# A two-layer decoder on one core: the FFN's 256-column chunk with gate and up in one matmul, two new banks for the last columns, and another order of the attention steps

## The chip, the cores and the metric

The kernel runs on one core of one Trainium2 chip. The metric is the device time of one execution in microseconds (us); lower is better. Engines are named as in the profile: PE (TensorE matmuls), PEld (its weight loads), DVE (VectorE), ACT (ScalarE), POOL (GpSimd), SP (SyncE, which issues most DMAs).

## What is computed

```python
for i in range(2):                      # x: 256 tokens x 1024
    h = rmsnorm(x, norm_mix[i]); mem_n = rmsnorm(mem, norm_mem[i])
    mix, mem_q = gmlp_mixer(h, ...) if i == 0 else nsa_mixer(h, ...)
    mem_o = mem_cross_attention(mem_q, mem_n, w_mem_kv[i])   # 4 heads, 256 memory tokens
    x = x + concatenate([mix, mem_o]) @ w_out
    h = rmsnorm(x, norm_ffn[i])
    x = x + (silu(h @ wg[i]) * (h @ wu[i])) @ wd[i]          # d_ff 2816
return rmsnorm(x, norm_final)
```

All data are float32. Layer 0 mixes tokens with a gated MLP (gMLP), whose spatial weights are 12 causal 128x128 matrices; layer 1 has attention (NSA) with 12 heads in 4 groups and three gated branches: compressed blocks, selected blocks and a window.

## The kernel before

A float32 matmul is made of three passes of a faster type. Every operand is split into a high part H and the rest L, and `mm3` (L228 to L230) adds aH·bH, aL·bH and aH·bL in one PSUM bank. `split` makes the high part on ACT (L122) and the rest on DVE (L123). So each piece of a weight (1024 columns) costs ACT one `wH` and DVE one `wL`, and each activation an `aH` and an `aL`. In the trace, H and L of an attention or FFN result are written `aH`, `aL` or `mid`.

Weights come as tiles of 1 MB (`Raw`, three buffers) from DMAs that SP issues. There are seven buffers each for `wH` and `wL`: a piece can be split when the piece seven before it has had its last use, which is in token block 1 (`tb`, 128 tokens each; there are two).

PE runs its program in the order in which the code issues it. This order is written by hand: `flow` advances a clock by an estimate for each matmul, and a spawned chain that says `yield 2.4` goes on when that clock is 2.4 us later. ACT, DVE and POOL run what a tile scheduler ordered by priority; `tc.high_priority(offset=...)` moves what is issued in it ahead.

The parts that the change touches:

- **FFN.** 2816 hidden columns in six chunks: first the 256 columns from 2560, then five of 512. For each chunk and token block `gate` multiplies into one bank and takes SiLU from it (L447, ACT); `up` multiplies into another and spawns `turn`, which takes the product (L451, DVE), transposes it after `yield 1.6` (L244, x2 or x4) and splits it. `down` then adds the chunk to four accumulators (2 token blocks x 2 halves of 512 columns) that stay open over all chunks. In the first chunk the order is gate, up for block 0, then gate, up for block 1.
- **Attention.** For each of six head pairs m there are three steps: `scores` (L925 to L929, then maxima on DVE, exponentials on ACT at L949, scaling on POOL at L954 and DVE), `turn` (12 transposes of probabilities and one of the compressed ones, `pcx`, L244; then copies L974, L980, L983 on ACT), and `attend` (L1001, with the split `aH`, `aL` of its result). `mixed(m, tb)` multiplies a finished result with its part of the output weights (two halves, 3 passes each; the `mm` tiles in lines L228 to L230 of the profile) and adds to accumulators of the next residual.
- **Compression** (layer 1): two hidden layers; SiLU of the first (L808, ACT), `yield 3.0`, two transposes, the second layer.
- **gMLP**: `v_chain` transposes the spatial weights (L660 and L661, three sets of four groups), then mixes set by set (`spatial`, L639); `yield 0.8` stands behind each set of transposes.
- **Memory attention**: copies of transposed probabilities on ACT (L412).
- **The end**: `final` adds the residual (L306, DVE), takes the sum of squares (L249, ACT), multiplies with the norm's weights (L1085, DVE), and when both halves are there takes the reciprocal root (L257, L258, POOL), scales (L1092 DVE, L1094 ACT) and stores with two DMAs of SP (L1095).

Of the kernel before, what the change touches and what calls it, by code (L numbers as in the profile page):

```python
# [11 lines left out]
AF = mybir.ActivationFunctionType  # L12
ALU = mybir.AluOpType
# [4 lines left out]
D = 1024  # L18
# [39 lines left out]


HI = 150  # L60
MEMLAT = 9.0
MEMCH = 0.0
VCH = 2.0
# [4 lines left out]
def body(tc, t, out):  # L68
    nc = tc.nc
    PE, ACT, DVE, POOL, SP = nc.tensor, nc.scalar, nc.vector, nc.gpsimd, nc.sync  # L70
    with ExitStack() as ctx:
# [233 lines left out]
            xs = x[:, tb, half * 512 : (half + 1) * 512]  # L305
            DVE.tensor_tensor(xs, acc, xs, op=ALU.add)  # L306

        def down(accs, act, ks, ws, first, last, after=None, tbs=(0, 1)):

            for tb in tbs:  # L310
                for half in range(2):
                    acc = accs[tb][half]
                    for i, k in enumerate(ks):
                        mm3(acc, st(act, k, tb), ws[i](slice(half * 512, (half + 1) * 512)),
                            first and i == 0, last and i == len(ks) - 1)
                        if tb == 1 and half == 1:
                            ws[i].done()
                    if after:
                        after(acc, tb, half)
# [61 lines left out]
        def mem_attention(qTs, tb, kv, dst, done):  # L381
# [26 lines left out]
            for i in range(2):  # L408
                pt = tr()
                transposes(pt, parts[i].rearrange("p j n -> p (j n)"), 4)  # L410
                pT = small([128, 4, 128])
                ACT.copy(pT, kview(pt, 4))  # L412
                pTs.append(pT)
            yield 3.2
            o = tr()
# [11 lines left out]
        def ffn_weights(layer):  # L427
            wg, wu, wd = t["ffn_w_gate"][layer], t["ffn_w_up"][layer], t["ffn_w_down"][layer]
            out = []
            for c0, n in [(2560, 256)] + [(i * 512, 512) for i in range(5)]:  # L430
                out.append((n // 128, w_in(wg, c0, n), w_in(wu, c0, n),
                            sum([cols(wd, c0 // 128 + k, 2, 0, D) for k in range(0, n // 128, 2)], [])))
            return out

        def ffn(weights, nrm, after):
            accs = [[mm(), mm()], [mm(), mm()]]
            for ci, (nk, wg, wu, wd) in enumerate(weights):
                n = nk * 128
                sil = [None, None]
                act = mid([128, 4, SEQ], F32R), mid([128, 4, SEQ], F32R)  # L440

                def gate(tb):
                    ps = tr()
                    gemm(ps, nrm.act, tb, wg, n)
                    sil[tb] = small([128, n])
                    with tc.high_priority(offset=HI):
                        ACT.activation(sil[tb], ps[:, :n], AF.Silu, scale=nrm.rstd[tb])  # L447

                def turn(ps, tb, act=act, sil=sil, n=n, nk=nk):
                    h = small([128, n])  # L450
                    DVE.scalar_tensor_tensor(h, ps[:, :n], nrm.rstd[tb], sil[tb], op0=ALU.mult, op1=ALU.mult)  # L451
                    yield 1.6
                    pt = tr()
                    transposes(pt, h, nk)
                    split(act[0][:, :nk, blk(tb)], act[1][:, :nk, blk(tb)], kview(pt, nk))

                def up(tb):
                    ps = tr()
                    gemm(ps, nrm.act, tb, wu, n)
                    flow.spawn(turn(ps, tb))  # L460
                    flow.tick(0)

                for f, tb in ((gate, 0), (up, 0), (gate, 1), (up, 1)) if nk == 2 else ((gate, 0), (gate, 1), (up, 0), (up, 1)):
                    f(tb)
                last = ci == len(weights) - 1
                end = lambda *a: flow.spawn(after(*a))
                down(accs, act, range(nk), wd, ci == 0, last, end if last else None)
            return accs


# [177 lines left out]
        def v_chain():  # L648
# [9 lines left out]
            for q in range(3):  # L658
                ps = tr()
                transposes(ps, wsr[:, q * 4 : q * 4 + 4, :].rearrange("p g s -> p (g s)"), 4)  # L660
                ACT.copy(wsT[:, q * 4 : q * 4 + 4, :], kview(ps, 4))  # L661
                yield 0.8
            for q in range(3):
                spatial(q)
                yield 1.0
# [98 lines left out]
        def compress():  # L764
# [41 lines left out]
            POOL.memset(hS, 0.0)  # L806
            for s in range(2):
                ACT.activation(hS[s * 64 : s * 64 + 60, :], ph[s * 64 : s * 64 + 60, 0:256], AF.Silu)  # L808
            yield 3.0
            pt = tr()  # L810
            transposes(pt, hS, 2)
            hTk = small([128, 2, 60])
# [173 lines left out]
        def attend(m):  # L986
            pT0, pT1 = turned[m]
            o = tr()
            for tb in range(2):
                n = 3 if tb == 0 else 5  # L990
                for i in range(n):
                    for hh in range(2):
# [6 lines left out]
                        else:  # L999
                            w, z = V[:, i // 2, i % 2, c], pT1[hh][:, i, :]  # L1000
                        PE.matmul(o[hh * 64 : hh * 64 + 64, blk(tb)], w, z, start=i == 0, stop=i == n - 1)  # L1001
            split(mix1[0][:, m, :], mix1[1][:, m, :], o[:, 0:256])

        soft, turned = {}, {}

# [7 lines left out]


        def step(f, *a):
            with tc.high_priority(offset=HI):
                f(*a)

        ps = mm()
# [35 lines left out]
        step(turn, 2)  # L1055
        mixed((1, 0))
        step(scores, 4)
        mixed((0, 1))
        step(attend, 2)
        step(turn, 3)  # L1060
        mixed((2, 0))
        step(scores, 5)
        mixed((1, 1))
        step(attend, 3)
        step(turn, 4)
        mixed((3, 0))
        step(attend, 4)
        step(turn, 5)
        mixed((4, 0), (2, 1))
        step(attend, 5)  # L1070
        mixed((3, 1), (5, 0), (4, 1), (5, 1))
        flow.until(lambda: f1.rstd[0] is not None)
# [2 lines left out]
        SP.dma_start(nf, t["norm_final"].partition_broadcast(128))  # L1075
        oview = out[0].rearrange("(b p) d -> p b d", p=128)
        sse = [tiny([128, 2], "ss") for _ in range(2)]

        def final(acc, tb, half):

# [15 lines left out]
            return  # L1096
            yield

        xgs = []
        ffn(WF1, f1, final)  # L1100
        flow.until(lambda: len(xgs) == 4)


_INS = [
# [33 lines left out]
```

## Time and profile before

| | |
|---|---|
| median of 3 runs | 637.43 us (636.39 to 638.38) |
| the profiled execution | 638.98 us, of which its span is 637.3 us |
| mean granted TensorE clock in it | 0.994 |
| PE busy | 97% of the span |

The span is the time from the first to the last record of the profile; the rest of the execution's time lies around it. [...] A matmul's duration in a row is longer than its pitch, the time from its start to the next one's start, since matmuls overlap in the engine.

### The profile page before, as it was taken

The numbers are of one execution on the slowest core, as the hardware profiler recorded it, in microseconds if no ns is written. First come the engines' busy times: TensorE is split into PE (matmuls) and PEld (weight loads), VectorE is DVE, ScalarE is ACT, GpSimd is POOL, SyncE is SP. The second block draws the span as 40 slices with busy tenths as digits, with TensorE's granted clock in tenths as the row PEclk, the third lists the DMA queues.
The fourth block names the chain that finished last, engine by engine and source line by source line (L and its number), as shares of the span: only waits on it lengthen the run. The fifth ranks groups of instructions, "written<-read, shape, count | busy, mean of one in ns | idle before, by whom it ended". The sixth has DMA issues, their size and how long they took to land.

```text
span 637.3 us, 8843 instructions
## 1 busy us (share of the span) xinstructions
PE 618.8 (97%) x3382; PEld 512.1 (80%) x3382; DVE 377.1 (59%) x616; ACT 327.0 (51%) x553; POOL 58.1 (9%) x90
## 2 busy tenths in 40 slices
PE   8999999999999999999999999889999999999995
PEld 6879879888888888889876786668988888888884
DVE  4898457463645545476597489746644545546344
ACT  5785567443535344365544479746543535344333
POOL 0330111000000000002003106420000000000001
PEclk9999999999999999999999999989999999999998
DMA  7966254565555564744948552042554554636401
GB/s 239 374 225 230 74 190 141 198 202 192 162 188 182 172 224 136 260 132 121 354 140 273 123 134 61 8 145 87 198 181 150 205 191 162 234 134 231 163 0 66
DMA packets 57330, 109.69 MB, mean 172 GB/s; under 512 B 3428, under 2 KB 19400, under 8 KB 57288
## 3 DMA queue, kind: packets, MB, share of 16 engines
q1 hardware_dynamic: 57272, 109.12, 51.4%
q8 instruction: 26, 0.43, 0.3%
q14 instruction: 16, 0.13, 0.1%
q10 hardware_dynamic: 16, 0.00, 0.0%
HBM read 108.07 MB, written 1.05 MB: 171 GB/s over the span
## 4 chain that ended last, share of the span: by engine, by line
PE 84%; ACT 5%; DMA 4%; DVE 4%; issue 1%; POOL 1%; SPq 0%; POOLq 0%; ACTq 0%; DVEq 0%
PE tr L229 13%; PE mm L228 13%; PE mm L229 13%; PE tr L230 13%; PE tr L228 13%; PE mm L230 12%; PE tr L244 4%; ACT mid L949 3%; DMA wsr<-in_gmlp_w_s_dram 2%; DMA x<-in_x_dram 1%; PE tr L798 1%; DVE wL L123 1%; DMA raw<-in_w_mem_kv_dram 1%; DVE wL L128 1%; PE tr L388 1%
## 5 line engine op out<-in xcount | busy, mean ns | idle before, releaser
L123 DVE TENSOR_TENSOR wL<-raw,wH 128x1024 fp32r<-128x1024 f32 (+1 forms) x170 | 207.0, 1236 | 148.8 <-ACT wH L122 142.9
L122 ACT CAST wH<-raw 128x1024 fp32r<-128x1024 f32 (+1 forms) x170 | 173.8, 1043 | 150.3 <-PE tr L229 75.5
L228 PE MATMUL tr<-wH,aH 128*128 128x512 f32 (+1 forms) x384 | 143.8, 375 | 0.0
L229 PE MATMUL tr<-wH,aL 128*128 128x512 f32 (+1 forms) x384 | 142.8, 372 | 0.6 <-DVE aL L123 0.6
L230 PE MATMUL tr<-wL,aH 128*128 128x512 f32 (+1 forms) x384 | 142.7, 372 | 0.0
L228 PE MATMUL mm<-wH,aH 128*128 128x512 f32 (+2 forms) x224 | 87.4, 390 | 0.0
L229 PE MATMUL mm<-wH,aL 128*128 128x512 f32 (+2 forms) x224 | 83.4, 372 | 3.3 <-DVE aL L123 3.3
L230 PE MATMUL mm<-wL,aH 128*128 128x512 f32 (+2 forms) x224 | 83.3, 372 | 0.1
L229 PEld LDWEIGHTS tr<-wH,aL 128*128 128x128 f32 x384 | 72.4, 188 | 13.1 <-DVE aL L123 0.9
L230 PEld LDWEIGHTS tr<-wL,aH 128*128 128x128 f32 x384 | 72.3, 188 | 12.6
L228 PEld LDWEIGHTS tr<-wH,aH 128*128 128x128 f32 x384 | 72.3, 188 | 12.3
L228 PE MATMUL mm<-wH,mid 128*128 128x512 f32 (+1 forms) x208 | 79.2, 381 | 0.0
L229 PE MATMUL mm<-wH,mid 128*128 128x512 f32 (+1 forms) x208 | 77.9, 374 | 0.0
L230 PE MATMUL mm<-wL,mid 128*128 128x512 f32 (+1 forms) x208 | 77.8, 374 | 0.0
L228 PEld LDWEIGHTS mm<-wH,aH 128*128 128x128 f32 x224 | 42.6, 190 | 10.2 <-issue 4.5
L229 PEld LDWEIGHTS mm<-wH,aL 128*128 128x128 f32 x224 | 42.5, 190 | 9.8 <-DVE aL L123 4.2
L230 PEld LDWEIGHTS mm<-wL,aH 128*128 128x128 f32 x224 | 42.4, 189 | 7.8 <-DVE wL L128 0.5
L257 POOL TENSOR_SCALAR rstd<-ss 128x1 f32<-128x1 f32 x14 | 7.4, 526 | 435.4 <-ACT junk L249 431.2
L230 PEld LDWEIGHTS mm<-wL,mid 128*128 128x128 f32 x208 | 39.2, 188 | 7.1
L229 PEld LDWEIGHTS mm<-wH,mid 128*128 128x128 f32 x208 | 39.2, 189 | 6.9 <-DVE mid L123 0.5
L228 PEld LDWEIGHTS mm<-wH,mid 128*128 128x128 f32 x208 | 39.2, 188 | 6.7 <-ACT mid L122 0.4
L451 DVE SCALAR_TENSOR_TENSOR small<-tr,rstd,small 128x512 f32<-128x512 f32 (+1 forms) x24 | 16.9, 703 | 36.5 <-PE tr L230 36.5
(158 smaller groups left out, 649.9 us busy)
## 6 DMA issues: line engine op xcount, KB each, us to landing
raw<-in_ffn_w_down_dram SPq DMA_DIRECT2D x22, 1024.0 KB, 5.0
raw<-in_ffn_w_gate_dram SPq DMA_DIRECT2D x20, 1024.0 KB, 5.1
raw<-in_ffn_w_up_dram SPq DMA_DIRECT2D x20, 1024.0 KB, 5.1
raw<-in_nsa_w_in_dram SPq DMA_DIRECT2D x6, 1024.0 KB, 6.9
raw<-in_gmlp_w_in_dram SPq DMA_DIRECT2D x4, 1024.0 KB, 8.7
raw<-in_w_mem_kv_dram SPq DMA_DIRECT2D x4, 1024.0 KB, 5.8
raw<-in_gmlp_w_out_dram SPq DMA_DIRECT2D x4, 1024.0 KB, 6.7
raw<-in_nsa_w_out_dram SPq DMA_DIRECT2D x12, 256.0 KB, 5.0
```

What stands on the lines that cost most here:

```text
L122: ACT.copy(H, src)
L123: DVE.tensor_tensor(L, src, H.bitcast(F32), op=ALU.subtract)
L128: DVE.scalar_tensor_tensor(L, src, g, H.bitcast(F32), op0=ALU.mult, op1=ALU.subtract)
L228: PE.matmul(ps, aH, bH, start=first, stop=False)
L229: PE.matmul(ps, aL, bH, start=False, stop=False)
L230: PE.matmul(ps, aH, bL, start=False, stop=last)
L244: PE.transpose(ps[:, (at + j) * 128 : (at + j + 1) * 128], src[:, j * 128 : (j + 1) * 128], ident)
L257: POOL.tensor_scalar(r, ss[:, 0:1], ss[:, 1:2], EPS, op0=ALU.add, op1=ALU.add)
L388: PE.matmul(scs[i][:, j * 256 : (j + 1) * 256], qT[r, j, :], kv[r, j, :], start=True, stop=True)
L451: DVE.scalar_tensor_tensor(h, ps[:, :n], nrm.rstd[tb], sil[tb], op0=ALU.mult, op1=ALU.mult)
L798: PE.matmul(ph[s * 64 : s * 64 + 60, 0:256], X[s][:, k // 8, k % 8, :], w1[q, s][:, j, :], start=k == 0, stop=k == 15)
L949: ACT.activation(o, o, AF.Exp, bias=nb[:, i : i + 1], scale=-1.0, accum_out=sm[:, i : i + 1])
```

## The change

- In the FFN's first chunk gate and up of a token block are one matmul of 512 columns: the weights stand side by side (256 of each) in two raw tiles, and `gate_up` replaces `gate` and `up`. One bank holds both, SiLU reads its first half, `turn` its second. The four DMAs of 512 KB become parts of two tiles.
- In the last FFN, the accumulator of block 1's second half ends with the fifth chunk and gets its residual there. The sixth chunk's part of these 512 columns goes to two new banks of 256 columns, each with its own residual, sum of squares and product (`last`). The last scaled parts leave by two DMAs of SP and one of ACT's queue.
- The attention steps have another order. `attend` and `turn` follow `scores(4)` without `mixed(0, 1)` between them, and `mixed` comes a step later from there on. The copies of `turn` and the splits of `attend` have a higher priority (UP = 500 instead of HI = 150, and instead of none for the splits), as have the copies of memory attention.
- `yield 3.0` of the compression becomes 6.0, and the `yield 0.8` behind gMLP's third set of transposes 2.4.

```diff
 HI = 150
+UP = 500
 MEMLAT = 9.0
...
-        def down(accs, act, ks, ws, first, last, after=None, tbs=(0, 1)):
+        def down(accs, act, ks, ws, first, last, after=None, tbs=(0, 1), parts=None, ends=False):
...
                     acc = accs[tb][half]
+                    if parts and tb == 1 and half == 1:
+                        for j in range(2):
+                            quarter = tr()
+                            for i, k in enumerate(ks):
+                                mm3(quarter[:, 0:256], st(act, k, tb), ws[i](slice(512 + j * 256, 768 + j * 256)),
+                                    i == 0, i == len(ks) - 1)
+                            parts(quarter, j)
+                        for w in ws:
+                            w.done()
+                        continue
                     for i, k in enumerate(ks):
                         mm3(acc, st(act, k, tb), ws[i](slice(half * 512, (half + 1) * 512)),
-                            first and i == 0, last and i == len(ks) - 1)
+                            first and i == 0, (last or (ends and tb == 1 and half == 1)) and i == len(ks) - 1)
                         if tb == 1 and half == 1:
...
                 pT = small([128, 4, 128])
-                ACT.copy(pT, kview(pt, 4))
+                with tc.high_priority(offset=UP):
+                    ACT.copy(pT, kview(pt, 4))
                 pTs.append(pT)
...
             for c0, n in [(2560, 256)] + [(i * 512, 512) for i in range(5)]:
-                out.append((n // 128, w_in(wg, c0, n), w_in(wu, c0, n),
+                if n == 256:
+                    both = []
+                    for k0 in (0, 4):
+                        loads = []
+                        for j, w in enumerate((wg, wu)):
+                            src = w[k0 * 128 : k0 * 128 + 512, c0 : c0 + n].rearrange("(k p) n -> p k n", p=128)
+                            loads.append((lambda r, j=j: r[:, :, j * 256 : j * 256 + 256], src))
+                        both += Raw([128, 4, 512], loads).kts
+                gates = both if n == 256 else w_in(wg, c0, n)
+                out.append((n // 128, gates, None if n == 256 else w_in(wu, c0, n),
                             sum([cols(wd, c0 // 128 + k, 2, 0, D) for k in range(0, n // 128, 2)], [])))
...
-        def ffn(weights, nrm, after):
+        def ffn(weights, nrm, after, parts=None):
             accs = [[mm(), mm()], [mm(), mm()]]
...
-                for f, tb in ((gate, 0), (up, 0), (gate, 1), (up, 1)) if nk == 2 else ((gate, 0), (gate, 1), (up, 0), (up, 1)):
+                def gate_up(tb):
+                    ps = tr()
+                    gemm(ps, nrm.act, tb, wg, 512)
+                    sil[tb] = small([128, n])
+                    with tc.high_priority(offset=HI):
+                        ACT.activation(sil[tb], ps[:, :n], AF.Silu, scale=nrm.rstd[tb])
+                    flow.spawn(turn(ps[:, n : 2 * n], tb))
+                    flow.tick(0)
+
+                for f, tb in ((gate_up, 0), (gate_up, 1)) if nk == 2 else ((gate, 0), (gate, 1), (up, 0), (up, 1)):
                     f(tb)
...
                 end = lambda *a: flow.spawn(after(*a))
-                down(accs, act, range(nk), wd, ci == 0, last, end if last else None)
+                if last and parts:
+                    residual(accs[1][1], 1, 1)
+                down(accs, act, range(nk), wd, ci == 0, last, end if last else None, parts=parts if last else None,
+                     ends=bool(parts) and ci == len(weights) - 2)
             return accs
...
                 ACT.copy(wsT[:, q * 4 : q * 4 + 4, :], kview(ps, 4))
-                yield 0.8
+                yield 0.8 if q < 2 else 2.4
             for q in range(3):
...
                 ACT.activation(hS[s * 64 : s * 64 + 60, :], ph[s * 64 : s * 64 + 60, 0:256], AF.Silu)
-            yield 3.0
+            yield 6.0
             pt = tr()
...
                         PE.matmul(o[hh * 64 : hh * 64 + 64, blk(tb)], w, z, start=i == 0, stop=i == n - 1)
-            split(mix1[0][:, m, :], mix1[1][:, m, :], o[:, 0:256])
+            with tc.high_priority(offset=UP):
+                split(mix1[0][:, m, :], mix1[1][:, m, :], o[:, 0:256])
...
         def step(f, *a):
-            with tc.high_priority(offset=HI):
+            with tc.high_priority(offset=UP if f is turn else HI):
                 f(*a)
...
         step(scores, 4)
-        mixed((0, 1))
         step(attend, 2)
         step(turn, 3)
+        mixed((0, 1))
+        step(scores, 5)
         mixed((2, 0))
-        step(scores, 5)
-        mixed((1, 1))
         step(attend, 3)
         step(turn, 4)
-        mixed((3, 0))
+        mixed((1, 1), (3, 0))
         step(attend, 4)
         step(turn, 5)
-        mixed((4, 0), (2, 1))
+        mixed((2, 1), (4, 0))
         step(attend, 5)
...
         sse = [tiny([128, 2], "ss") for _ in range(2)]
+        sst = [tiny([128, 1], "sst") for _ in range(2)]
...
+        def last(quarter, j):
+
+            c = slice(512 + j * 256, 768 + j * 256)
+            xs = x[:, 1, c]
+            DVE.tensor_tensor(xs, quarter[:, 0:256], xs, op=ALU.add)
+            sumsq(xs, sst[j], D)
+            if j == 0:
+                POOL.tensor_scalar(sst[0], sst[0], sse[1][:, 0:1], EPS, op0=ALU.add, op1=ALU.add)
+            xg = small([128, 256])
+            DVE.tensor_tensor(xg, xs, nf[:, c], op=ALU.mult)
+            xgs.append(xg)
+            if j == 1:
+                r = tiny([128, 1], "rstd")
+                POOL.tensor_tensor(r, sst[0], sst[1], op=ALU.add)
+                POOL.tensor_tensor(r, r, neghalf, op=ALU.pow)
+                xa, xb, xc = xgs[-3:]
+                DVE.tensor_scalar(xc, xc, r, None, op0=ALU.mult)
+                ACT.activation(xa, xa, AF.Copy, scale=r)
+                SP.dma_start(oview[:, 1, c], xc)
+                DVE.tensor_scalar(xb, xb, r, None, op0=ALU.mult)
+                ACT.dma_start(oview[:, 1, 0:512], xa)
+                SP.dma_start(oview[:, 1, 512:768], xb)
+
         xgs = []
-        ffn(WF1, f1, final)
-        flow.until(lambda: len(xgs) == 4)
+        ffn(WF1, f1, final, last)
+        flow.until(lambda: len(xgs) == 5)
 _INS = [
```

PE's program around attention's step 2, in the kernel before (mid and pcx are probabilities, mm an output accumulator):

```order
L925 MATMUL tr<-KT,QT 128x271 x2
L927 MATMUL tr<-KT,QT 128x15 x2
L929 MATMUL tr<-KT,QT 128x512 x2
L228 MATMUL mm<-wH,aH 128x512
L229 MATMUL mm<-wH,aL 128x512
L230 MATMUL mm<-wL,aH 128x512
L228 MATMUL mm<-wH,aH 128x512
L229 MATMUL mm<-wH,aL 128x512
L230 MATMUL mm<-wL,aH 128x512
L1001 MATMUL tr<-mid,V 64x128 x4
L1001 MATMUL tr<-pcx,vc 64x128 x2
```

And in the changed kernel, where the lines have moved by 33 (L925 is L958, L1001 is L1034) or 1 (L228 is L229, L244 is L245):

```order
L958 MATMUL tr<-KT,QT 128x271 x2
L960 MATMUL tr<-KT,QT 128x15 x2
L962 MATMUL tr<-KT,QT 128x512 x2
L1034 MATMUL tr<-mid,V 64x128 x4
L1034 MATMUL tr<-pcx,vc 64x128 x2
L1034 MATMUL tr<-mid,V 64x128 x8
L1034 MATMUL tr<-pcx,vc 64x128 x2
L245 MATMUL tr<-ident,mid_3686 128x128 x2
L245 MATMUL tr<-ident,mid_3703 128x128 x2
L245 MATMUL tr<-ident,mid_3686 128x128 x4
L245 MATMUL tr<-ident,mid_3703 128x128 x4
L245 MATMUL tr<-ident,pcx 128x128
```

The six `mm` passes between `scores(4)` and `attend(2)` are gone from this place; they come behind `turn(3)`, which ends with the transpose of `pcx`.

ACT's program at attention's steps 2 and 3, before: the end of the exponentials (L949, L961), then a weight piece, the split of attend's result and turn's copies:

```order
L949 ACTIVATE mid_3857,sm_3864<-mid_3857,nb_3858 128x256 x2
L961 ACTIVATE pcx<-pcx 128x4x15
L122 CAST wH<-raw 128x1024
L122 CAST aH<-tr 128x256
L974 COPY mid<-tr 128x512
L980 COPY mid<-tr 128x512 x2
L983 COPY pcx<-tr 128x128
```

And changed, at the same step (L949 is L982, L961 is L994, L974 to L983 are L1007 to L1016, L122 is L123):

```order
L982 ACTIVATE mid_3805,sm_3812<-mid_3805,nb_3806 128x256 x2
L123 CAST aH<-tr 128x256
L994 ACTIVATE pcx<-pcx 128x4x15
L1007 COPY mid<-tr 128x512
L1013 COPY mid<-tr 128x512 x2
L1016 COPY pcx<-tr 128x128
L123 CAST wH<-raw 128x1024
```

The split `aH` has gone ahead of the compressed exponential, and the weight piece `wH` behind the three copies.

ACT's program in the first FFN's first chunk, before (tb 0's SiLU with its table load, tb 0's split `mid`, tb 1's SiLU, tb 1's split):

```order
L447 ACT_TABLE_LOAD
L447 ACTIVATE small<-tr,rstd 128x256
L122 CAST aH<-small 128x4x128
L122 CAST wH<-raw 128x1024
L122 CAST mid<-tr 128x2x128
L122 CAST wH<-raw 128x1024
L447 ACTIVATE small<-tr,rstd 128x256
L122 CAST wH<-raw 128x1024 x2
L122 CAST mid<-tr 128x2x128
```

And changed (SiLU is L489 now; L468 would be the next chunk's):

```order
L489 ACT_TABLE_LOAD
L489 ACTIVATE small<-tr,rstd 128x256
L123 CAST wH<-raw 128x1024
L123 CAST mid<-tr 128x2x128
L123 CAST wH<-raw 128x1024 x3
L489 ACTIVATE small<-tr,rstd 128x256
L123 CAST mid<-tr 128x2x128
```

Four weight pieces stand ahead of the second SiLU, where there were two since the first.

## Rows read from the trace of the kernel before

**Rows 1.** The page's part 1: busy time, share of the span, instructions.
```profile
PE 618.8 (97%) x3382; PEld 512.1 (80%) x3382; DVE 377.1 (59%) x616; ACT 327.0 (51%) x553; POOL 58.1 (9%) x90
```

**Rows 2.** PE's waits: line, releaser: sum in us, number, longest.
```profile
PE mm L229 <- DVE aL L123: 3.3, 2, 1.6
```

**Rows 3.** Timeline at the first long wait: start, us, engine line; [idle before <-releaser].
```profile
410.69 1.03 ACT L122 CAST wH<-raw 128x1024 fp32r<-128x1024 f32 x1
...
411.62 0.36 ACT L122 CAST aH<-tr 128x256 fp32r<-128x256 f32 x1
...
412.26 2.08 DVE L123 TENSOR_TENSOR wL<-raw,wH 128x1024 fp32r<-128x1024 f32 x1
...
412.51 0.14 PEld L244 LDWEIGHTS tr<-ident,pcx 128*128 128x128 f32 x1 [0.31 <-ACT mid L974]
...
412.60 0.48 PE L228 MATMUL mm<-wH,aH 128*128 128x512 f32 x1
...
414.73 0.77 PE L229 MATMUL mm<-wH,aL 128*128 128x512 f32 x1 [1.65 <-DVE aL L123]
```

**Rows 4.** Windows: us, busy per engine (instructions), PEclk, DMA share, GB/s.
```profile
415.00:418.00 3.00, 3.00 (x9) 1.95 (x10) 0.00 (x0) 0.00 (x0) 0.00 (x0) 0.50 0.86 268
```

**Rows 5.** Timeline at the second long wait.
```profile
426.68 0.50 PE L229 MATMUL mm<-wH,aL 128*128 128x512 f32 x1 [1.65 <-DVE aL L123]
```

**Rows 6.** Timeline of scores(3), attend(1), turn(2): first and last.
```profile
397.68 0.73 PE L925 MATMUL tr<-KT,QT 64*128 64x271 f32 x4
...
404.04 0.33 PE L244 MATMUL tr<-ident,pcx 128*128 128x128 f32 x1 [1.00 <-DVE aL L123]
```

**Rows 7.** Timeline at the compression's second layer.
```profile
352.55 0.39 PE L230 MATMUL mm<-wL,aH 128*128 128x512 f32 x1
...
353.77 0.41 PE L244 MATMUL tr<-ident,small 128*128 128x128 f32 x2 [0.83 <-issue]
```

**Rows 8.** Timeline at gMLP's first spatial mix.
```profile
45.89 0.40 PE L230 MATMUL mm<-wL,aH 128*128 128x512 f32 x1
...
47.21 0.60 PE L639 MATMUL tr<-Vv,wsT 128*128 128x128 f32 x3 [0.92 <-ACT wsT L661]
```

**Rows 9.** Windows of gMLP's second half: us, PE, PEld, DVE, ACT, POOL busy.
```profile
50.00:60.00 10.00, 10.00 (x88) 9.85 (x87) 10.00 (x17) 6.02 (x9) 0.00 (x0) 1.00 0.61 223
```

**Rows 10.** Timeline: twelve 256-wide passes of FFN 0, 14 512-wide passes of FFN 1.
```profile
107.12 0.28 PE L228 MATMUL tr<-wH,aH 128*128 128x256 f32 x1
...
108.44 0.28 PE L230 MATMUL tr<-wL,aH 128*128 128x256 f32 x1
...
627.20 0.39 PE L229 MATMUL mm<-wH,mid 128*128 128x512 f32 x1
...
630.14 0.39 PE L230 MATMUL mm<-wL,mid 128*128 128x512 f32 x1
```

**Rows 11.** Timeline of FFN 0's first chunk: SiLU's table load, SiLU, product, transposes.
```profile
104.12 1.28 ACT L447 ACT_TABLE_LOAD   x1 [0.31 <-PE tr L230]
...
105.42 0.47 ACT L447 ACTIVATE small<-tr,rstd 128x256 f32<-128x256 f32 x1
...
107.04 0.48 DVE L451 SCALAR_TENSOR_TENSOR small<-tr,rstd,small 128x256 f32<-128x256 f32 x1
...
112.45 1.23 DVE L123 TENSOR_TENSOR wL<-raw,wH 128x1024 fp32r<-128x1024 f32 x1 [0.21 <-ACT wH L122]
```

**Rows 12.** Timeline of the tail, after the last matmul.
```profile
630.57 0.69 DVE L306 TENSOR_TENSOR x<-mm,x 128x512 f32<-128x512 f32 x1 [1.05 <-PE mm L230]
...
631.35 0.63 ACT L249 ACTIVATE junk<-x 128x512 bf16<-128x512 f32 x1 [1.74 <-DVE x L306]
...
633.13 0.49 DVE L1092 TENSOR_SCALAR small<-small,rstd 128x512 f32<-128x512 f32 x1 [1.15 <-POOL rstd L258]
```

**Rows 13.** Groups of instructions by form: busy, mean ns of one, idle before.
```profile
L249 ACT ACTIVATE junk<-Vv 128x256 bf16<-128x256 f32 x2 | 0.8, 410 | 0.0
...
L743 DVE TENSOR_TENSOR small<-mm,cs 128x256 f32<-128x256 f32 x8 | 3.4, 419 | 4.4 <-PE mm L230 4.4
```

## The prediction

> **What bounds the kernel now.** I read the page's part 1 first: PE is busy for 97% of the span, DVE and ACT for little over half [rows 1]. So the time can fall in two ways only: fewer or cheaper matmul passes, or fewer stalls of PE. The stalls are some 18 us of the span, and the view of PE's waits says who ends them. Its largest item is the second of the three passes in `mixed`, which waits twice for an `aL` from DVE [rows 2]. I then followed each stall that the change touches in the timeline (rows 3 to 8), and the first chunk of the FFN and the tail (rows 10 to 12), where the change alters work itself.
>
> **Attention.** The chain at the first long wait reads like this [rows 3]: ACT takes a weight piece `wH` at 410.69 ahead of `aH` (411.62); DVE takes the piece's `wL` at 412.26 ahead of `aL`, and this one lasts 2.08 us, because POOL works at the same time. PE starts the first pass of `mixed` at 412.60, and its second only at 414.73: 2.13 us for a pitch of 0.23, a loss of 1.90. [...] At the next step the same wait returns with the same 1.65 us idle and no loss of clock behind it [rows 5]: 1.90 again. Ahead of each the `pcx` transpose waits for a copy, 0.31 in these rows, and I take 0.3 for each. In all 1.90 + 1.8 + 1.90 + 0.6 = 6.2 us are to be had.
>
> The new order of ACT takes the cause away: `aH` comes right behind the exponentials and `wH` behind the copies; on DVE `wL` then follows `aL`. And `mixed`, which waited, now uses results one step older. What it costs: `scores(4)`, `attend(2)`, `turn(3)` follow each other without six passes between them. The trace shows this pattern once, at `scores(3)`, `attend(1)`, `turn(2)`: from 397.68 to the last transpose at 404.04, which waited 1.00 us for an `aL` behind the exponentials [rows 6]. I charge 1.2 us for a second such place. Net: -6.2 + 1.2 = -5.0. Bounds: -6.2 if the new place does not wait; -2.5 if only one of the two long waits goes and the clock still falls once, as both copies and exponentials keep ACT fully busy there.
>
> **Compression.** PE starts a pass at 352.55 and goes on at 353.77, because SiLU on ACT is late [rows 7]: 1.22 less a pitch of 0.23, 0.99 us lost. With 3 us more of other work put ahead of the transposes (five `mm3`, twelve transposes and more, all ready by the order), it goes: -1.0. What follows the second layer is late by as much, but it feeds attention only after the query transposes; I see no waiter, and give ±0.3.
>
> **gMLP.** The first mix starts at 47.21 after a pass at 45.89 [rows 8]: 1.09 us lost, and this goes too, as four `mm3` come ahead. But DVE is busy for 10.00 of the 10.00 us behind it [rows 9], and in its changed order the first product u·mixed comes behind one more weight piece and the third mix. I work out that it ends near 56.9, where PE reaches its transposes near 55.9. So the loss comes back: -0.1; ends -1.09 and +0.3. The copies in memory attention change places with weight pieces within short waits of PE that stay: 0, within ±0.5.
>
> **FFN, the first chunk.** Passes: twelve 256-wide ones start 0.120 us apart (107.12 to 108.44), fourteen 512-wide ones 0.226 apart (627.20 to 630.14) [rows 10]. 96 passes become 48: 11.52 becomes 10.86, -0.66 for each FFN. [...]
>
> Against this stand two new waits. Before, SiLU of gate ran under the passes of up. Now both wait for the same last pass. (a) Block 0: from the start of a bank's last pass to its reader 0.43 us (630.14 to 630.57, [rows 10, 12]), the load and the start of SiLU behind it 1.30, SiLU 0.47, the step to DVE about 0.10, the product 0.48 [rows 11]: 2.78. By the order PE has three `mm3`, nine passes of 0.226, between this last pass and the pair of transposes, and is there after 2.26. So 0.5 is lost. (b) Block 1: ACT's order puts the fourth `wH` ahead of the second SiLU, and DVE's the fourth `wL` (1.23 us, [rows 11]) ahead of the product. This `wH` waits for the weight's last use, in the same passes that SiLU waits for; `wH` (1.03, [rows 3]), `wL` and the product follow one another on two engines with no gap: 0.2 + 1.03 + 0.06 + 1.23 + 0.48 = 3.0 against PE's 2.3. So 0.6 to 0.7 is lost. Together +1.15 less 0.66: +0.5 an FFN, **+1.0** for two. Ends: -1.3 if neither wait appears, +2 if the pieces behind are late too.
>
> **Tail.** Quarters: 24 passes of 0.120 for 12 of 0.226, +0.17, but the last pass is 0.11 shorter. Behind it, the residual falls from 0.69 to 0.42 [rows 12, 13], the sum of squares from 0.63 to 0.41, the last scaling (0.49) to some 0.3, about 0.7 in all; of SP's stores one goes through ACT's queue. POOL's two instructions stay on the path. What the last DMA needs to land doesn't shrink with it, and half of the gain may go there: I take -0.5, from -0.8 to +0.3.
>
> **Sum.** -5.0 -1.0 -0.1 +0 +1.0 -0.5 = -5.6 us. Against the profiled execution, 638.98 us (span 637.3), this gives 633.4. The profiled execution stands 1.55 above the median of 637.43; the same sum from the median gives 631.8. The half-clock stretch may be in that execution and not in each of the others. I take the middle, **632.6 us**.
>
> **The rivals.** What a measurement can tell from no change is 0.3%, 1.9 us: faster means under 635.5, slower over 639.3.
>
> 1. *The attention wait moves and stays half as large.* ACT is busy for the whole of two stretches there, and the bundle scores-attend-turn has nothing between it for PE. `attend(2)`, `turn(3)` and `turn(4)` would each wait 1 us, as `turn(2)` does [rows 6]. Gain there 2.5 instead of 5.0: 635.1.
> 2. *The waits in the FFN's first chunk or in gMLP don't come.* They are differences of 0.5 to 1 us between two chains of several steps. Without (a) and (b), and with half of gMLP's 1.09: 632.6 - 2.4 - 0.5, and a little more from the tail: 629.7 to 630.5.
> [...]
> 4. *The other side: weight pieces starve.* UP moves copies and splits ahead of pieces on ACT and DVE. A piece costs ACT 1.03 and DVE up to 2.08 us [rows 3]. If the FFN that follows finds its four first pieces and the output weights' three not split, 7 x 1.03 = 7.2 us of ACT work would lie on the path, more than the 5.6 gained, and with the waits that the late pieces then cause in the next chunk 639.3 or more. It decides from seven pieces on. ACT's order speaks against: it has a piece between the bundles still.
> 5. *The change does nothing in attention*: the two waits come again at other places in full, because DVE beside POOL is as slow as before, and the clock falls again. Then 632.6 + 5.0 = 637.6.
>
> **How the numbers follow.** The forecast has 0.50 (631.0 to 634.2, its own range); rival 1 0.16, rival 2 0.16, rival 3 0.06, rival 4 0.03, rival 5 0.09. Faster: 0.50, 0.16, most of rival 1 (0.13), half of rival 3 (0.03) and part of rival 5 (0.03), 0.85; same 0.12; slower 0.03. The range leaves out rivals 4 and 5 and the outer parts of 1 to 3: 629.8 to 635.8.
>
> **What would show it.** In the changed kernel's profile: no wait for `aL` over 0.5 us at `mixed(2, 0)` and `mixed(3, 0)`, and a granted clock of 1.00 through attention; waits of 0.3 and 1.2 at `attend(2)` and `turn(3)`; waits of about 0.5 and 0.7 at the pair of transposes in the first chunk of both FFNs; one of about 1.0 near 56 at gMLP's product; no gap at 353; and the last DMA's issue some 0.5 nearer to the last pass. The prediction is wrong if the clock falls at a new place, or if a wait for `wL` stands where none was: at the second FFN's begin above all.

## The result and the profile after

The changed kernel takes 633.88 us in the median (633.83 to 634.47, 4 runs) against 637.12 before (636.39 to 638.38, 4 runs) on the same chip: ratio 0.9948, 95% interval 0.9936 to 0.9960, so 3.3 us faster. The forecast was 632.6, from 629.8 to 635.8. The profiled execution takes 634.47 us with a span of 632.7, 4.5 us and 4.6 us less than the profiled one of before.

PE's waits in the changed kernel (line, releaser: sum in us, number, longest); line numbers have moved by 1 in the helpers and by more behind them:

```profile
PE tr L245 <- DVE aL L124: 2.5, 3, 1.0
PE tr L245 <- DVE small L472: 2.0, 4, 0.6
PE tr L112 <- DVE warm L103: 1.1, 1, 1.1
PE tr L245 <- DMA x<-in_x_dram: 1.1, 1, 1.1
PE tr L245 <- DVE small L704: 0.9, 1, 0.9
```

The two waits of `mixed` for `aL` [rows 2, 3, 5] are gone from the list. Three shorter ones stand in their place, all at turn's `pcx` transpose, and four new ones for `small` from L472, the product of the FFN's first chunk. The timeline gives their places, with SiLU and its table load in the FFN's first chunk; the first row is the transposes of gMLP's product:

```profile
56.21 0.52 PE L245 MATMUL tr<-ident,small 128*128 128x128 f32 x3 [0.86 <-DVE small L704]
...
105.93 1.28 ACT L489 ACT_TABLE_LOAD   x1 [2.11 <-PE tr L231]
107.22 0.47 ACT L489 ACTIVATE small<-tr,rstd 128x256 f32<-128x256 f32 x1
107.50 0.39 PE L231 MATMUL tr<-wL,aH 128*128 128x512 f32 x1
107.73 0.48 DVE L472 SCALAR_TENSOR_TENSOR small<-tr,rstd,small 128x256 f32<-128x256 f32 x1 [1.69 <-ACT small L489]
108.27 0.33 PE L245 MATMUL tr<-ident,small 128*128 128x128 f32 x1 [0.38 <-DVE small L472]
...
111.97 1.06 ACT L123 CAST wH<-raw 128x1024 fp32r<-128x1024 f32 x1 [0.32 <-PE tr L230]
112.93 0.47 ACT L489 ACTIVATE small<-tr,rstd 128x256 f32<-128x256 f32 x1
113.06 1.23 DVE L124 TENSOR_TENSOR wL<-raw,wH 128x1024 fp32r<-128x1024 f32 x1
113.81 0.39 PE L231 MATMUL mm<-wL,mid 128*128 128x512 f32 x1
114.20 0.48 DVE L472 SCALAR_TENSOR_TENSOR small<-tr,rstd,small 128x256 f32<-128x256 f32 x1
114.82 0.41 PE L245 MATMUL tr<-ident,small 128*128 128x128 f32 x2 [0.63 <-DVE small L472]
...
403.39 0.33 PE L245 MATMUL tr<-ident,pcx 128*128 128x128 f32 x1 [1.00 <-DVE aL L124]
...
411.21 0.33 PE L245 MATMUL tr<-ident,pcx 128*128 128x128 f32 x1 [0.99 <-DVE aL L124]
...
420.08 0.33 PE L245 MATMUL tr<-ident,pcx 128*128 128x128 f32 x1 [0.48 <-DVE aL L124]
```

In block 0 of the first chunk the transposes come 0.77 us after the pass before them, 0.54 more than a pitch of 0.23. ACT had been idle for 2.11 us when the table load began, and the row has PE's last pass for this bank as what released it: so the load's 1.28 us stand on this path, and no run tries the load earlier. In block 1 the order forecast is there: `wH` (111.97) ahead of SiLU (112.93), `wL` (113.06) ahead of the product (114.20), and PE loses 1.01 less 0.23 = 0.78. At the `pcx` transposes the list's 1.00, 0.99 and 0.48 are idle time; from the start of the last transpose before (402.12, 409.95, 419.33), less a pitch of 0.11, PE loses 1.16, 1.15 and 0.64. The first one stood in the kernel before too [rows 6].

Windows of the changed kernel's attention (us, busy of PE, PEld, DVE, ACT, POOL, PEclk, DMA share, GB/s), which answer to [rows 4]:

```profile
400.00:403.00 3.00, 2.39 (x30) 1.98 (x25) 2.02 (x12) 3.00 (x14) 1.61 (x2) 1.00 0.00 0
...
409.00:412.00 3.00, 2.01 (x16) 1.69 (x14) 2.03 (x9) 2.98 (x10) 2.62 (x4) 1.00 0.01 3
412.00:415.00 3.00, 3.00 (x19) 1.67 (x18) 1.86 (x3) 1.05 (x1) 0.60 (x1) 1.00 0.02 5
415.00:418.00 3.00, 3.00 (x38) 2.42 (x36) 2.89 (x23) 2.71 (x13) 0.08 (x1) 1.00 0.57 150
```

The clock is 1.00 all through. Where PE waits (400 to 403, 409 to 412), ACT is busy for the whole time.

The tail after, which answers to [rows 12]:

```profile
626.26 0.28 PE L231 MATMUL tr<-wL,mid 128*128 128x256 f32 x1
...
626.58 0.43 DVE L1137 TENSOR_TENSOR x<-tr,x 128x256 f32<-128x256 f32 x1 [0.40 <-PE tr L231]
...
627.10 0.42 ACT L250 ACTIVATE junk<-x 128x256 bf16<-128x256 f32 x1 [0.77 <-DVE x L1137]
...
628.61 0.35 DVE L1149 TENSOR_SCALAR small<-small,rstd 128x256 f32<-128x256 f32 x1 [1.15 <-POOL rstd L1147]
...
629.37 0.43 SPq L1154 DMA_DIRECT2D out_dram<-small  x1
```

From the last pass to the last scaling there are 2.35 us now and 2.99 before (630.14 to 633.13, [rows 10, 12]).

**The ledger by stage.** Each stage is the difference of two PE starts in a kernel's trace: "first chunk" from the FFN's first pass to the first pass of its second chunk; "to attention" from the last pass of layer 1's memory keys and values, which follow FFN 0 (300.00 in the kernel before), to the first pass of `scores`; "attention" from there to FFN 1's first pass; "end" from FFN 1's second chunk to the end of the span. Microseconds, one profile each:

| kernel | first chunk, FFN 0 | to attention | attention | first chunk, FFN 1 | end |
|---|---|---|---|---|---|
| before | 18.18 | 77.69 | 65.20 | 19.47 | 174.94 |
| before, second profile | 18.20 | 77.64 | 65.22 | 19.47 | 174.92 |
| changed | 19.05 | 76.95 | 60.94 | 20.23 | 174.51 |
| old attention (e1) | 19.05 | 76.93 | 65.11 | 20.17 | 174.54 |
| gate and up apart (e2) | 18.16 | 76.98 | 60.90 | 19.44 | 174.54 |
| gMLP's 0.8 (e3) | 19.11 | 77.15 | 60.91 | 20.21 | 174.61 |
| old compression (e4) | 19.05 | 77.63 | 60.92 | 20.21 | 174.51 |
| old end (e5) | 19.06 | 76.93 | 60.91 | 20.20 | 174.89 |
| new FFN order (e6) | 17.63 | 76.95 | 60.91 | 18.79 | 174.56 |
| new attention order (e7) | 19.06 | 76.90 | 57.82 | 20.24 | 174.55 |
| both new orders (e8) | 17.73 | 76.93 | 57.82 | 18.85 | 174.48 |
| only attention changed (e9) | 18.13 | 77.64 | 60.92 | 19.44 | 174.87 |
| zero matmuls in the waits (e10) | 19.06 | 76.95 | 66.51 | 20.16 | 174.59 |
| memory's copies as before (e11) | 19.11 | 76.93 | 60.93 | 20.21 | 174.54 |

Spans are read to 0.1 us, so the last column holds to about 0.05. A stage that an experiment doesn't touch keeps its length within 0.1 us in this table (0.2 in one cell, 77.15), so no action of one part on another shows. Against before: +0.87, -0.74, -4.26, +0.76, -0.4, in all -3.8. Between the first two stages all these profiles take 181.25 to 181.31. What is left of the span's difference lies ahead of the first FFN (the load of x ended 0.57 earlier in the changed kernel's profile). The two profiles of the same kernel before already differ by 0.9 us up to there, and that part isn't resolved.

### The profile page after: what moved, and what is told of

Read it like the earlier page. It is cut to its first block, busy times and chain, and to the rows that moved or that the text cites. A ratio compares the mean times of both kernels' runs of the same rounds, so it can differ in the third digit from the quotient of the medians.

```text
span 632.7 us, 8684 instructions
## 1 busy us (share of the span) xinstructions
PE 616.5 (97%) x3298; PEld 507.6 (80%) x3298; DVE 378.0 (60%) x620; ACT 328.0 (52%) x555; POOL 59.4 (9%) x91
## 4 chain that ended last, share of the span: by engine, by line
PE 81%; ACT 7%; DVE 5%; DMA 5%; issue 1%; SPq 0%; POOL 0%; POOLq 0%; ACTq 0%; DVEq 0%
PE tr L230 13%; PE tr L229 13%; PE tr L231 13%; PE mm L229 12%; PE mm L230 12%; PE mm L231 12%; PE tr L245 4%; DMA raw<-in_gmlp_w_in_dram 3%; ACT mid L982 3%; PE tr L831 1%; DMA raw<-in_w_mem_kv_dram 1%; DVE wL L129 1%; ACT wH L123 1%; DVE wL L124 1%; ACT wH L128 1%
## 5 line engine op out<-in xcount | busy, mean ns | idle before, releaser
L123 ACT CAST wH<-raw 128x1024 fp32r<-128x1024 f32 (+1 forms) x170 | 173.6, 1043 | 146.3 <-PE tr L230 71.6
L229 PE MATMUL tr<-wH,aH 128*128 128x512 f32 x352 | 138.4, 393 | 0.0
L230 PE MATMUL tr<-wH,aL 128*128 128x512 f32 x352 | 137.1, 390 | 0.5 <-DVE aL L124 0.5
L231 PE MATMUL tr<-wL,aH 128*128 128x512 f32 x352 | 137.2, 390 | 0.0
L229 PE MATMUL mm<-wH,aH 128*128 128x512 f32 (+2 forms) x224 | 86.9, 388 | 0.0
L230 PEld LDWEIGHTS tr<-wH,aL 128*128 128x128 f32 x352 | 66.2, 188 | 14.3 <-DVE aL L124 0.9
L229 PE MATMUL mm<-wH,mid 128*128 128x512 f32 (+1 forms) x204 | 77.5, 380 | 0.0
L231 PEld LDWEIGHTS tr<-wL,aH 128*128 128x128 f32 x352 | 66.1, 188 | 14.1
L229 PEld LDWEIGHTS tr<-wH,aH 128*128 128x128 f32 x352 | 66.1, 188 | 13.3
L230 PE MATMUL mm<-wH,mid 128*128 128x512 f32 (+1 forms) x204 | 76.3, 374 | 0.0
L231 PE MATMUL mm<-wL,mid 128*128 128x512 f32 (+1 forms) x204 | 76.1, 373 | 0.0
L229 PEld LDWEIGHTS mm<-wH,aH 128*128 128x128 f32 x224 | 42.5, 190 | 9.5 <-issue 4.0
L230 PEld LDWEIGHTS mm<-wH,mid 128*128 128x128 f32 x204 | 38.5, 189 | 6.6 <-DVE mid L124 0.5
L229 PEld LDWEIGHTS mm<-wH,mid 128*128 128x128 f32 x204 | 38.5, 189 | 6.6 <-ACT mid L123 0.4
L472 DVE SCALAR_TENSOR_TENSOR small<-tr,rstd,small 128x512 f32<-128x512 f32 (+1 forms) x24 | 16.9, 704 | 39.6 <-PE tr L231 35.4
```

Of the source, the lines that this page charges most:

```text
L123: ACT.copy(H, src)
L229: PE.matmul(ps, aH, bH, start=first, stop=False)
L230: PE.matmul(ps, aL, bH, start=False, stop=False)
L231: PE.matmul(ps, aH, bL, start=False, stop=last)
```

## The experiments

**1. Attention as before**, the rest changed: the diff's hunk on the steps taken back, `turn` at HI, `split` without priority.

```diff
         step(scores, 4)
+        mixed((0, 1))
         step(attend, 2)
         step(turn, 3)
-        mixed((0, 1))
-        step(scores, 5)
         mixed((2, 0))
...
```

> The changed kernel with attention's steps in the order of before and without the raised priority of turn and attend's split; all else as changed. By the ledger of the two profiles attention gave 4.26 us, of which about 1.8 is the stretch at half clock: a profile with two waits of 1.65 us for aL, and 4.3 us slower than the changed kernel if the clock falls again (638.2), 2.5 slower if it doesn't (636.4). By the rival, that the change got its time elsewhere (the first load of x came 0.57 us earlier, and the executions of before differ by 2 us among themselves): under 1.5 us slower.

Measured: 638.31 us (12 runs), 1.0013 of the kernel before (1.0000 to 1.0025). So without attention's new order (and its priorities) the change gains nothing. The stage returns to 65.11, with both waits and the half clock behind the first. Rows and windows of its profile, columns as above:

```profile
411.69 0.48 PE L229 MATMUL mm<-wH,aH 128*128 128x512 f32 x1
413.82 0.49 PE L230 MATMUL mm<-wH,aL 128*128 128x512 f32 x1 [1.65 <-DVE aL L124]
...
423.49 0.47 PE L229 MATMUL mm<-wH,aH 128*128 128x512 f32 x1
425.70 0.50 PE L230 MATMUL mm<-wH,aL 128*128 128x512 f32 x1 [1.74 <-DVE aL L124]
```

```profile
412.00:415.00 3.00, 1.35 (x5) 1.01 (x5) 1.76 (x2) 0.67 (x3) 0.35 (x1) 0.90 0.18 21
415.00:418.00 3.00, 3.00 (x14) 1.73 (x13) 0.58 (x6) 0.24 (x1) 0.00 (x0) 0.53 0.90 328
...
424.00:427.00 3.00, 1.30 (x5) 0.86 (x5) 1.65 (x2) 0.48 (x2) 0.23 (x1) 1.00 0.56 175
```

**2. Gate and up apart again**, the rest changed (loads and order of the first chunk as before).

```diff
-                for f, tb in ((gate_up, 0), (gate_up, 1)) if nk == 2 else
+                for f, tb in ((gate, 0), (up, 0), (gate, 1), (up, 1)) if nk == 2 else
```

> The changed kernel with the first FFN chunk's gate and up apart again, in both FFNs. By the prediction's step (the two waits of 0.54 and 0.78 us cost more than the passes save) and the ledger (0.7 and 0.8 us lost): 1.4 us faster than the changed kernel, 632.4, and no wait over 0.2 us at the chunk's transposes. By the rival, that fewer passes pay and the waits only move to the next chunk: 1.3 us slower, 635.2.

Measured: 632.71, 0.9925 (0.9910 to 0.9941). This is 0.23% under the changed kernel's ratio; the intervals overlap, but the stages don't leave it open: both return to 18.16 and 19.44. The wide matmul as it was put in costs 0.89 and 0.79 us.

**3 and 4. gMLP's 0.8 and compression's 3.0 again**, one at a time.

```diff
-                yield 0.8 if q < 2 else 2.4
+                yield 0.8
```

```diff
-            yield 6.0
+            yield 3.0
```

> The changed kernel with 0.8 in place of 2.4 behind gMLP's third set of transposes. By the prediction the wait only moves, from the first spatial mix (1.09) to the first product (1.02): the same within 0.3 us, and the profile shows the first wait again and not the second. By the rival, that the two places have each its own cause: both waits, 1 us slower; or none.

> The changed kernel with 3.0 in place of 6.0 before the compression's transposes. By the prediction 0.99 us of wait for SiLU come back; by the ledger, which shows 0.74 up to attention, 0.7 slower: 634.6. By the rival, that what follows is late by as much, 0.0 to 0.2.

Measured: gMLP 634.10, 0.9945 (0.9930 to 0.9960), not to be told from the changed kernel. In its timeline the first mix waits again, though less than before, and the first product's transposes (54.04) don't; a small wait comes later. So the wait did not move back whole. One profile doesn't size it either: with the changed kernel's gMLP code the product's wait is 0.2 us in experiment 7's profile and 1.0 in experiment 2's.

```profile
45.67 1.16 PE L672 MATMUL tr<-Vv,wsT 128*128 128x128 f32 x8 [0.33 <-ACT wsT L694]
...
54.04 0.60 PE L245 MATMUL tr<-ident,small 128*128 128x128 f32 x4
...
56.76 0.44 PE L245 MATMUL tr<-ident,small 128*128 128x128 f32 x2 [0.25 <-DVE small L724]
```

Compression: 634.67, 0.9957 (0.9941 to 0.9972); its stage is 77.63 against 76.95, so the longer `yield` is worth 0.7, as expected from the ledger.

**5. The end as before.** `ffn(WF1, f1, final)` without `last`.

> The changed kernel with the end of before: the last chunk's second half in its accumulator, no quarters, all stores by SP. By the prediction and the ledger the new end gives 0.5 us (0.25 more up to the last pass, 0.72 less behind it): 634.4. By a rival from the other experiments, in which the parts other than attention come to 0.8 us of loss together, more than their single terms: the new end costs 0.3 to 0.6 us, 633.4.

Measured: 634.77, 0.9963 (0.9951 to 0.9975). The end is 174.89 against 174.51: the new one gives 0.4 us, near the 0.5 forecast. The rival, that it costs time, falls.

**6. The wide matmul with SiLU's chain freed.** Block 0's transposes come one `mm3` later, and each block's last `mm3` uses the high part of the weight last, so that in block 1 the fourth piece isn't free earlier than SiLU's bank.

```diff
+            if wh_last:
+                PE.matmul(ps, aH, bL, start=False, stop=False)
+                PE.matmul(ps, aL, bH, start=False, stop=False)
+                PE.matmul(ps, aH, bH, start=False, stop=last)
...
-                    yield 1.6
+                    yield 2.4 if nk == 2 and tb == 0 else 1.6
...
-                    gemm(ps, nrm.act, tb, wg, 512)
+                    gemm(ps, nrm.act, tb, wg, 512, wh_last=True)
```

> The changed kernel with gate and up still in one matmul, but block 0's transposes one mm3 later (yield 2.4) and, in the chunk's last mm3 of block 1, the two passes with wH behind the one with wL, so that the fourth weight piece isn't free before SiLU's bank is, and SiLU and the product come first in ACT's and DVE's order. If the two waits are what the chunk costs, both go and the passes' saving stays: 2 x (0.54 + 0.78) = 2.6 us faster than the changed kernel, 631.3, and 1.4 faster than with gate and up apart. By the rival, that SiLU's chain is too long in any order (table load, or the down passes wait for the split instead): no faster than gate and up apart, 632.7.

Measured: 631.58, 0.9909 (0.9892 to 0.9925). The stages are 17.63 and 18.79: 1.42 and 1.44 under the changed kernel, and 0.53 and 0.65 under gate and up apart. Its timeline in block 1, in the order forecast:

```profile
110.81 0.47 ACT L494 ACTIVATE small<-tr,rstd 128x256 f32<-128x256 f32 x1 [0.59 <-PE tr L232]
111.18 1.04 ACT L123 CAST wH<-raw 128x1024 fp32r<-128x1024 f32 x1
111.59 0.48 DVE L477 SCALAR_TENSOR_TENSOR small<-tr,rstd,small 128x256 f32<-128x256 f32 x1
...
112.25 1.23 DVE L124 TENSOR_TENSOR wL<-raw,wH 128x1024 fp32r<-128x1024 f32 x1 [0.18 <-ACT wH L123]
...
112.60 0.38 PE L250 MATMUL tr<-ident,small 128*128 128x128 f32 x2
```

SiLU and the product come ahead of the piece's `wH` (111.18) and `wL` (112.25), and PE doesn't wait. The 1.4 us gained are no less than the two waits (0.54 + 0.78). So the waits were the whole cost, and the order of two engines the cause of the second. The two parts of the edit were not tried apart.

**7 and 8. A third order of attention**, alone and with the new FFN: `mixed` of block 1 between `attend` and the next `turn`.

```diff
         step(attend, 1)
+        mixed((0, 1))
         step(turn, 2)
         mixed((1, 0))
         step(scores, 4)
         step(attend, 2)
+        mixed((1, 1))
         step(turn, 3)
-        mixed((0, 1))
-        step(scores, 5)
         mixed((2, 0))
+        step(scores, 5)
         step(attend, 3)
+        mixed((2, 1))
         step(turn, 4)
...
```

> The changed kernel with attention's order changed once more: six passes of mixed of block 1 between attend and the next turn (steps 1 to 3), so that the waits of 1.22, 1.21 and 0.70 us before the pcx transposes are covered. By the ledger up to 3.1 us faster: 630.8. By the rival, that ACT and DVE are the bound of these steps (fully busy) and PE only waits elsewhere, or that mixed of block 0 waits for aL again as in the kernel before: the same, 633 to 635.

> The FFN's and attention's new versions together. If the two are apart, the gains add: 628 to 629 if both hold.

Measured: 631.09, 0.9909 (0.9891 to 0.9926), and together 628.55 (628.09 to 628.93), 0.9864 (0.9847 to 0.9882): 8.5 us under the kernel before, faster than both kernels by intervals that don't meet. The stage falls by 3.12, of which the three waits (1.16 + 1.15 + 0.64) are 2.95; the sizes expected had too short a pitch taken off. PE is busy throughout in the windows of experiment 7:

```profile
400.00:412.00 12.00, 12.00 (x100) 9.55 (x97) 9.65 (x43) 10.51 (x37) 6.16 (x8) 1.00 0.28 89
412.00:424.00 12.00, 12.00 (x117) 9.56 (x116) 8.70 (x33) 8.07 (x28) 3.51 (x5) 1.00 0.23 66
```

**9. Attention's new order alone, in the kernel before.**

> The kernel before with nothing but attention's new order of steps (no priorities, no other part). If the order alone makes the whole gain of attention: 3.5 to 4.4 us faster than the kernel before, 633 to 633.5, and the spread of its executions shrinks from 3 us to about 1, since no half-clock stretch is left. By the rival, that the raised priorities do part of it: 2 us faster or less, with waits for aL left.

Measured: 633.99, 0.9945 (0.9926 to 0.9965), and the stage is 60.92 as in the changed kernel. So the order of PE's steps makes all of it. The raised priority does nothing there: from the first `scores` to FFN 1, ACT, DVE and POOL run the same instructions in the same order in the traces with it (changed) and without (experiment 9). That the spread shrank isn't shown (633.23 to 635.03); of the six executions five have a mean granted clock of 0.997 or 0.998, and the slowest has 0.994.

**10. The waits filled with matmuls by zeros**, in the kernel of experiment 1; `fill[0]` is 15 at the two places and 0 elsewhere.

```diff
             PE.matmul(ps, aH, bH, start=first, stop=False)
+            for _ in range(fill[0]):
+                PE.matmul(ps[:, 0:128], warm, warm, start=False, stop=False)
```

> The kernel of the first experiment (old order of attention) with 15 matmuls of 128 columns by zeros, which add zero, behind the first pass at each of the two places where PE waits for aL: PE is busy where it idled, and nothing is waited for differently. If the idle is what takes the clock down: the granted clock stays 1.00 from 412 to 420, and it is 1.5 to 1.8 us faster than without them, 636.6, with a smaller spread. By the rival, that the clock falls for another cause, or that the extra passes cost their own time: 638.3 or slower, clock 0.5 for 3 us again.

Measured: 640.12, 1.0043 (1.0027 to 1.0059). The time misses, the clock answers. Rows of the timeline and windows of this kernel:

```profile
412.47 0.48 PE L231 MATMUL mm<-wH,aH 128*128 128x512 f32 x1
412.78 3.51 PE L233 MATMUL mm<-warm 128*128 128x128 f32 x30
416.05 0.48 PE L235 MATMUL mm<-wH,aL 128*128 128x512 f32 x1
```

```profile
412.00:415.00 3.00, 2.92 (x25) 2.64 (x24) 2.54 (x3) 1.45 (x4) 1.12 (x2) 1.00 0.01 3
415.00:418.00 3.00, 3.00 (x25) 2.44 (x23) 0.00 (x0) 0.00 (x0) 0.00 (x0) 1.00 0.82 261
```

Each of these float32 matmuls is two passes (x30), so they took 3.58 us where the wait took 2.13 (411.69 to 413.82 in experiment 1): 1.45 too long at each place. Yet the way from the first filled place to the second (412.47 to 424.30) is 11.83 us against 11.80 in experiment 1 (411.69 to 423.49). So the clock that stayed at 1.00 gave back what the first filling overran: the half clock is worth about 1.45 us, and it comes from the idle before it. The other executions agree: in all eight of this kernel the mean granted clock is 0.997 or more, in seven of experiment 1's twelve it is 0.995 or less.

**11. Memory attention's copies without the raised priority.**

> The changed kernel without the raised priority of memory attention's copies. By the prediction 0 within 0.5 us: 633.4 to 634.4. By a rival, which would close the sum of the single parts: the priority costs 0.5 to 1 us, 633.

Measured: 634.67, 0.9958 (0.9944 to 0.9972): 0.1% above the changed kernel's ratio, with intervals that overlap, so not to be told from it, and not the gain that the rival asked for. The part ahead of the first FFN varies by more.

**12. A second profile of the kernel before.**

> The kernel before once more, for a second profile. If the half-clock stretch is what makes its executions differ by 3 us, its length differs from the first profile's, and the span with it; if every execution has it alike, the same within 0.3 us.

Measured: 638.09, span 636.4, and the half clock is there as in the first (windows):

```profile
412.00:415.00 3.00, 1.35 (x4) 0.99 (x4) 1.77 (x2) 0.68 (x3) 0.35 (x1) 0.82 0.28 30
415.00:418.00 3.00, 3.00 (x16) 1.75 (x14) 0.27 (x3) 0.00 (x0) 0.00 (x0) 0.61 0.79 322
```

0.18 and 0.39 of 3 us each make 1.7 us lost. The attention stages of the two profiles are 65.20 and 65.22, so these two executions don't differ there. Others do, by their clocks. The three profiles with this stretch (before, 1 and 12) have a mean granted clock of 0.994, all profiles without it 0.997 to 0.999. Of the 50 executions of the kernel before that were taken beside the experiments, 28 have 0.994 to 0.996, with a median of 638.0 us, and 22 have 0.997 or 0.998, with 636.6 (apart by 1.1 to 1.7 on each of the three chips). So the stretch is likely in little more than half of them, and the 1.5 us between the groups fit its price. That is argued, not shown: no profile of the second group was taken, and a mean doesn't say where the clock fell (with attention's new order 5 of 62 executions have 0.996 or less, too).

## Why the prediction was right, and where its sizes were off

- **Attention, forecast -5.0 (-6.2 to -2.5), measured -4.26.** Mechanism and place are shown by experiments 1 and 9: the two waits go, and the clock with them. What was mis-sized is the charge for the new order, 1.2 us for one new place. `turn(3)` did lose 1.15, and `turn(4)` another 0.64 (420.08), which the sum left out; rival 1 had named it. No run shows the 1.8 that the sum has for the clock's part; it is 1.45 (experiment 10) to 1.7 (experiment 12) where the clock falls. That `wL` is slow beside POOL shows in the trace of the kernel before: where POOL is idle, a `wL` of 1024 columns takes 1.21 to 1.23 us; at 412.26 and 424.21 it takes 2.08, each time beside 1.00 us of a TENSOR_TENSOR on POOL; at 394.19, beside the first of a pair of them, it kept 1.22, and POOL's pair (from 394.44) took 2.43 instead of 1.61.
- **The FFN's first chunk, forecast +0.5 each, measured +0.87 and +0.76.** Both waits came, at 0.54 and 0.78 against 0.5 and 0.6 to 0.7. The passes' gain was put at 0.66; experiment 6, without the waits, gets 0.53 in the first FFN and 0.65 in the second. The pitch of 0.226 was read at the end of the last FFN; in the first FFN's chunk the passes start 0.23 apart (107.27, 107.50).
- **Rival 3, the table load (0.06 among the chances).** No run shows it holding PE for longer than its own time: SiLU starts 1.29 us after the load's start in the changed kernel (105.93, 107.22), so nothing but the load's own 1.28 is on the path, and in the kernel before, ACT's idle time ahead of the load is 0.31 [rows 11].
- **Compression, forecast -1.0, measured -0.74** in its stage and given back by experiment 4. Why 0.25 of the 0.99 lost there doesn't come back isn't shown.
- **gMLP, forecast -0.1.** The new wait came at 56.21 (0.86 idle), forecast near 56, at about 1.0; taking the `yield` back changes nothing that can be measured.
- **The tail, forecast -0.5, measured -0.4** (experiment 5: 0.4). What the last store needs to land didn't shrink: a median of 2.2 us from its issue for SP's 256 KB before, 2.4 for the 256 KB on ACT's queue now (1.8 for SP's parts of 128 KB).
- **The base.** The forecast took the middle between the profiled execution and the median, in case the half clock is not in every execution. The clocks on record bear that out (experiment 12): all three profiles with the old order have the stretch, but only about half of the executions. So the stages, read from a profile that has it, overstate what the median gains: the -3.8 less half of 1.5 is about -3.1, beside the 3.3 measured. From the median, which holds the stretch by half, the forecast's sum with half of its 1.8 gives 632.7; the middle gave 632.6. What was wrong are the sizes: -5.6 against -3.8, of which attention has 0.7, the FFN 0.6 and compression 0.3. They err the same way; the time lies 1.3 above the forecast, inside a range that was 6 us wide.
- **Rivals 4 and 5** are out: no weight piece is late, and the attention did change.

## What to carry to other kernels

When passes on a saturated engine are merged, look for the reader that ran under the second half: here SiLU lost its cover, and the saving was smaller than the wait. A wait that vanished with the order of a stage left others behind here; the timeline of the nearest similar place gave the size of one of them (1.16 there, 1.15 at the new place), and a piece of independent work put exactly there took them away (experiments 7 and 8). The last use of a buffer can decide the order of what waits for it: SiLU had a raised priority before and after experiment 6, and what put it ahead of the weight piece there was the edit with the two passes swapped. One profile is one execution: where executions fall in two groups, look at every run's clock before a stage's gain is taken for the median's.

## What the runs showed of the hardware

After 1.65 us of idle time on PE (2.13 from start to start, in the kernel before and in experiment 1) the granted clock fell: its mean over 415 to 418 is 0.50 in the kernel before [rows 4], 0.53 and 0.61 in experiments 1 and 12, the three profiles with the old order, and it cost 1.45 to 1.7 us. A nearly equal idle time 12 us later (1.65 in the kernel before [rows 5], 1.74 in experiment 1) took nothing: the clock is 1.00 over 427 to 430 in the one and over 424 to 427 in the other. With PE kept busy by work without use (experiment 10) the clock stayed at 1.00 over 412 to 418. What tells the two places apart isn't settled by these runs, nor why the mean clocks show such a fall in only about half of the executions. A float32 matmul of 128 columns showed as two passes, 0.109 us each (3.27 us for 30).
